# Latent attention: transposes two heads and value products five heads behind the logits, with probability tiles in the big pool

## The chip, the cores and the metric

The kernel runs on one core of a Trainium2 chip. The metric is the device time of one execution in microseconds; the number given is the median of several runs. A core has five engines with their own queues: TensorE (PE; its weight loads are listed as PEld), VectorE (DVE), ScalarE (ACT), GpSimd (POOL) and SyncE (SP), which here issues most DMAs.

## What is computed

Two transformer networks of two layers each, one behind the other, on 256 tokens of width 1024, in float32. The change touches one mixer of the second network, a latent attention with 16 heads, in which every query sees every key:

```python
def mla_mixer(h, pos, w_in, g_qa, w_qb, g_kva, w_kvb, g_q, g_k, w_o):
    proj = h @ w_in
    q_lat = proj[..., :Q_LORA]
    kv_lat = proj[..., Q_LORA:Q_LORA + KV_LORA]
    k_rope = rope(proj[..., Q_LORA + KV_LORA:], pos)
    q = (rms_norm(q_lat, g_qa) @ w_qb).reshape(B, S, MLA_HEADS, MLA_QK)
    kv = (rms_norm(kv_lat, g_kva) @ w_kvb).reshape(B, S, MLA_HEADS, MLA_NOPE + MLA_V)
    ...
    q = rms_norm(q, g_q)
    k = rms_norm(k, g_k)
    o = dense_attention(q, k, v, MLA_QK ** -0.5)
    return o.reshape(B, S, MLA_HEADS * MLA_V) @ w_o
```

`dense_attention` takes, for each head, the softmax of q k^T times the scale, and multiplies it with v. A query or key has 96 elements in a head (64 and 32 rotated ones), a value has 64. Ahead of this mixer lie the whole first network (two layers with a causal attention of 8 heads); behind it lie the output projection, an MLP, a second layer with a dilated attention, and a second MLP.

## The kernel before

All weights stream from HBM in chunks of up to 2112 columns (`raw`, four slots). ScalarE casts a chunk to its upper part (`whi`, L313), VectorE subtracts to get the lower part (`wlo`, L314), and every product with a weight is three matmuls (L362 to L364 with the weight as the moving side, L366 to L368 with it stationary).

Tiles come from pools with a fixed number of slots; a tile takes a slot until its last reader is done. `big` (`bt()`) has 32 slots, `t2()` has 5, `t1()` 6. In PSUM there are two pools of four banks: `acc()` for products with weights and for value products, `att()` for logits and transposes. A planner orders the work of each engine: every instruction has a rank by the place where the program lists it, and an instruction whose inputs or slots are not there yet may be passed by one of lower rank. The order so found is fixed in the program, and each engine then works its queue in that order.

The latent attention treats its 16 heads in four groups. For a group, `proj_kv` (L1317) and `proj_q` (L1347) project values, keys and queries, `post_kv` (L1338) scales keys, and `tr_qk` (L1367) transposes one head's queries and keys on TensorE (L1372) and copies them to a big tile on ScalarE (L1374, L1375). The attention itself is a generator, `attn_std` (L650), that is also used, with `causal` set, by the first network. It has three steps for a head:

- `st0`: logits (L674), row maximum (L677) and its scaling (L678) on VectorE, exponentials with row sums on ScalarE (L640, two of them), reciprocal (L643) and the normalising multiply (L648, two of them) on VectorE. The result is a probability tile `p`.
- `st1`: four transposes of `p` on TensorE (L695), copied by ScalarE to a tile `pt` (L697).
- `st2`, for a pair of heads: eight value-product instructions on TensorE (L707, L711) into one `acc` bank, whose two halves of the partitions belong to the two heads, and the split of the result on ScalarE (L479) and VectorE (L480) into `oT`.

The loop at L717 lists, at step i, `st0` of head i, `st1` of head i - D1 and, every second step, `st2` of the pair that begins at head i - D2. It stops after each (`yield`), and the driver (L1435) puts other work between: the projections and transposes of the next groups at fixed yields (L1431), two units of the modulation (`ada0`, at yields 20 and 30), and from yield 23 on one block each of the output projection (`out_ahead`, L1398; 21 blocks into three `acc` banks, a block only when its heads' `st2` is listed).

Big tiles alive in this stage: 8 of `oT`, 2 and 3 of the key-value and query latents (until the last group is projected), one value tile for each group, four query and key tiles for each group until its last `tr_qk`, one tile for each transposed head until its logits are done.

Of the kernel before, what the change touches and what calls it, by code (L numbers as in the profile page):

```python
# [240 lines left out]
def tile_net(ctx, tc, wts, ada, xin, cols_in, table_in, fb_in, c_in, pos_in, inv_in, mask_in, freq_in, out):  # L241
# [17 lines left out]
    def mk(pool, shape, dt, tag, bufs=None):  # L259
        cnt[0] += 1  # L260
        kw = {} if bufs is None else {"bufs": bufs}
        return pool.tile(shape, dt, tag=tag, name=f"{tag}{cnt[0]}", **kw)

    def bt(shape=(128, 512), dt=F32):
        return mk(big, list(shape), dt, "b")
# [7 lines left out]
    def t2(shape=(128, 512), dt=F32):  # L273
        return mk(t2p, list(shape), dt, "t2")

    def sm(n=1):
        return mk(smp, [128, n], F32, "sm")

    def acc():
        return mk(accp, [128, 512], F32, "acc")  # L280

    def att():
        return mk(attp, [128, 512], F32, "att")
# [194 lines left out]
    def split_plain(dst, src):  # L478
        S.copy(out=dst[:, 0, :], in_=src)  # L479
        V.tensor_tensor(out=dst[:, 1, :], in0=src, in1=dst[:, 0, :].bitcast(F32), op=ALU.subtract)  # L480
# [155 lines left out]
    def softmax_tail(src, spans, nm, P, qs=None, act=False):  # L636

        rs = sm(len(spans))
        for i, (a, b) in enumerate(spans):
            S.activation(out=P[:, a:b], in_=src[:, a:b], func=AF.Exp, bias=nm[:, i:i + 1], scale=1.0 if qs is None else qs[i],  # L640
                         accum_out=rs[:, i:i + 1])
        rc = sm(len(spans))
        V.reciprocal(out=rc[:, :len(spans)], in_=rs[:, :len(spans)])  # L643
        for i, (a, b) in enumerate(spans):
            if act:
                S.activation(out=P[:, a:b], in_=P[:, a:b], func=AF.Copy, scale=rc[:, i:i + 1])
            else:
                V.tensor_scalar(out=P[:, a:b], in0=P[:, a:b], scalar1=rc[:, i:i + 1], scalar2=None, op0=ALU.mult)  # L648

    def attn_std(heads, qkT, vcol, oT, causal, qscale=None, done=set()):  # L650


        P, PT, O = {}, {}, {}
        D1, D2 = (3, 6) if causal else (1, 4)

        def st0(h_):
            qk = qkT(h_)
            ps = att()
            nm = sm(2)
            p = t2()  # L660
            if causal:
                PE.matmul(out=ps[:, :128], lhsT=qk[:, 0, :128], rhs=qk[:, 1, :128], start=True, stop=True)
                PE.matmul(out=ps[:, 128:384], lhsT=qk[:, 0, 128:], rhs=qk[:, 1, :], start=True, stop=True)
                spans = [(0, 128), (128, 384)]
                sc = t2()
                mx = sm(2)
                for i, (a, b) in enumerate(spans):
                    V.tensor_tensor_reduce(out=sc[:, a:b], in0=ps[:, a:b], in1=cmask[:, 256 - (b - a):], scale=1.0,
                                           scalar=-3e38, op0=ALU.add, op1=ALU.max, accum_out=mx[:, i:i + 1])
                V.tensor_scalar(out=nm[:, :2], in0=mx[:, :2], scalar1=-1.0, scalar2=None, op0=ALU.mult)  # L670
                src = sc
            else:
                for i in range(2):
                    PE.matmul(out=ps[:, 256 * i:256 * i + 256], lhsT=qk[:, 0, 128 * i:128 * i + 128], rhs=qk[:, 1, :], start=True, stop=True)  # L674
                spans = [(0, 256), (256, 512)]
                mx = sm(2)
                V.tensor_reduce(out=mx[:, :2], in_=ps.rearrange("p (a b) -> p a b", a=2), axis=AX.X, op=ALU.max, negate=True)  # L677
                V.tensor_tensor(out=nm[:, :2], in0=mx[:, :2], in1=qscale(h_), op=ALU.mult)  # L678
                src = ps
            softmax_tail(src, spans, nm, p, None if causal else [qscale(h_)[:, i:i + 1] for i in range(2)], causal)  # L680
            P[h_] = p

        def st1(h_):
            p = P.pop(h_)
            ps = att()
            pt = t2()
            if causal:
                PE.transpose(ps[:, 0:128], p[:, 0:128], ident)
                PE.transpose(ps[:, 128:256], p[:, 128:256], ident)
                PE.transpose(ps[:, 256:384], p[:, 256:384], ident)  # L690
                S.copy(out=pt[:, :384], in_=ps[:, :384])
            else:
                for kt in range(2):
                    for qt in range(2):
                        PE.transpose(ps[:, kt * 256 + qt * 128:kt * 256 + qt * 128 + 128],  # L695
                                     p[:, qt * 256 + kt * 128:qt * 256 + kt * 128 + 128], ident)
                S.copy(out=pt, in_=ps)  # L697
            PT[h_] = pt

        def st2(h0):  # L700
            ps = acc()
            for kt in range(2):
                for e in range(2):
                    pt = PT[h0 + e]
                    o_ = ps[64 * e:64 * e + 64, :256]
                    if kt == 0:
                        PE.matmul(out=o_, lhsT=vcol(h0 + e, 0), rhs=pt[:, 0:256], start=True, stop=False)  # L707
                    elif causal:
                        PE.matmul(out=o_[:, 128:256], lhsT=vcol(h0 + e, 1), rhs=pt[:, 256:384], start=False, stop=True)
                    else:  # L710
                        PE.matmul(out=o_, lhsT=vcol(h0 + e, 1), rhs=pt[:, 256:512], start=False, stop=True)  # L711
            split_plain(oT[h0 // 2], ps[:, :256])
            done.add(h0 // 2)
            del PT[h0], PT[h0 + 1]

        n = len(heads)
        for i in range(n + D2):  # L717
            if i < n:
                st0(heads[i])
                yield 600  # L720
            if D1 <= i < n + D1:
                st1(heads[i - D1])
                yield 400
            if i >= D2 and (i - D2) % 2 == 0 and i - D2 < n:
                st2(heads[i - D2])
                yield 500
# [87 lines left out]
    for l in range(2):  # L814
# [70 lines left out]
        def attn_side(qa=qa, vt=vt, e2=e2, oT=oT, l=l):  # L885
            ps = att()
            PE.matmul(out=ps[:, 0:8], lhsT=upper, rhs=e2[:, 0:8], start=True, stop=True)
            PE.matmul(out=ps[:, 8:16], lhsT=ones, rhs=e2[:, 0:8], start=True, stop=False)
            PE.matmul(out=ps[:, 8:16], lhsT=upper, rhs=e2[:, 8:16], start=False, stop=True)
            for tt in range(2):  # L890
                for hf in range(2):
                    V.tensor_scalar(out=qa[1, tt, hf][:, :, 64:65].rearrange("p a b -> p (a b)"),
                                    in0=ps[:, 8 * tt + 4 * hf:8 * tt + 4 * hf + 4], scalar1=-1.0, scalar2=None, op0=ALU.mult)
            yield 1200
            qkT = {}
            for hd in range(8):
                qkT[hd] = bt([128, 2, 256])
            for hd in range(8):
                ps = att()
                for wh in range(2):  # L900
                    for tt in range(2):
                        PE.transpose(ps[:, wh * 256 + tt * 128:wh * 256 + tt * 128 + 128], qa[wh, tt, hd // 4][:, hd % 4, :], ident)
                S.copy(out=qkT[hd][:, 0, :], in_=ps[:, :256])
                V.tensor_scalar(out=qkT[hd][:, 1, :], in0=ps[:, 256:], scalar1=gA[:, l:l + 1], scalar2=None, op0=ALU.mult)
                yield 720
            yield from attn_std(list(range(8)), lambda hd: qkT[hd], lambda hd, kt: vt[kt][:, hd * 64:hd * 64 + 64], oT, True)
# [517 lines left out]
    for g in range(4):  # L1424
# [4 lines left out]
        if g + 1 < 4:  # L1429
            ops += [(5 + e, lambda g=g, e=e: tr_qk(4 * g + 4 + e)) for e in range(4)]  # L1430
        todo += [(8 * g + n_, f) for n_, f in ops]  # L1431
    at = attn_std(list(range(16)), lambda hd: qkM.pop(hd), lambda hd, kt: vM[hd // 4][:, kt, (hd % 4) * 64:(hd % 4) * 64 + 64], oT, False,
                  lambda hd: rM[hd // 4].rearrange("p (t a) -> p a t", t=2)[:, hd % 4, :], done)
    ahead, ahead_done = None, []
# [224 lines left out]
```

## Time and profile before

| what | us |
|---|---|
| median of 3 runs | 1575.91 (1574.87 to 1577.45) |
| the profiled execution's own time | 1573.53 |
| its span in the trace | 1571.8 |
| TensorE busy in the span | 1547.1 |
| TensorE at 2.4 GHz: mean granted clock | 0.999 |

The page lists busy times for each engine over the span, the chain of work that ended last, and groups of instructions by line, engine and tile. The views of the trace give the same for a stretch of time: busy time in windows, who waited for whom, and the instructions of one engine in order of time. An engine's idle time is put down to what ended it.

### The profile page before, as it was taken

How to read it: one execution, taken by the hardware profiler on the slowest of the kernel's cores; microseconds unless marked ns; L12 is line 12 of the kernel's file. 1: busy time of each engine (PE TensorE's matmuls, PEld its weight loads, DVE VectorE, ACT ScalarE, POOL GpSimd, SP SyncE). 2: the span in 40 equal slices, each digit the busy share in tenths (PEclk: the TensorE clock that was granted, in tenths of full speed). 3: DMA queues.
4: the chain of work that ended last, by engine and by line, in shares of the span. 5: the costliest groups of instructions: out<-in, count | busy, mean ns of one | idle time of the engine just before them, and what ended most of it. 6: DMA issues, size and time to landing. Idle time of an engine off the chain costs nothing.

```text
span 1571.8 us, 31232 instructions
## 1 busy us (share of the span) xinstructions
PE 1547.1 (98%) x12314; PEld 1502.6 (96%) x12314; DVE 1189.0 (76%) x2430; ACT 899.6 (57%) x1854; POOL 233.8 (15%) x273
## 2 busy tenths in 40 slices
PE   8999999999999999999989999999999999999999
PEld 7999999999899999999977899999999999999999
DVE  7877877789787777778878688767777777686642
ACT  7474554442657454443258677533676766677632
POOL 1100100055210010006312000010223222110000
PEclk9999999999999999999999999999999999999999
DMA  8455666644655666664534277776766667655551
GB/s 315 168 188 202 219 240 221 235 170 155 222 195 188 230 221 228 220 241 162 173 124 155 84 244 265 266 283 224 223 211 215 220 201 238 196 205 185 192 198 41
DMA packets 83906, 320.68 MB, mean 204 GB/s; under 512 B 31984, under 2 KB 34816, under 8 KB 58928
## 3 DMA queue, kind: packets, MB, share of 16 engines
q1 hardware_dynamic: 83184, 317.30, 58.9%
q8 instruction: 97, 1.59, 0.4%
q0 software_dynamic: 432, 1.28, 0.2%
q14 instruction: 49, 0.40, 0.1%
q10 hardware_dynamic: 144, 0.11, 0.0%
HBM read 311.32 MB, written 7.34 MB: 203 GB/s over the span
## 4 chain that ended last, share of the span: by engine, by line
PE 87%; DVE 8%; issue 2%; POOL 1%; ACT 1%; DMA 1%; SPq 0%; ACTq 0%; POOLq 0%; DVEq 0%
PE acc L366 20%; PE acc L368 20%; PE acc L367 20%; PE acc L362 6%; PE acc L364 6%; PE acc L363 6%; DVE wlo L314 3%; POOL sm L405 1%; PE att L1541 1%; PE att L1543 1%; PE att L1555 1%; DVE oh L743 1%; PE att L674 1%; PE acc L707 1%; PE att L1572 1%
## 5 line engine op out<-in xcount | busy, mean ns | idle before, releaser
L314 DVE TENSOR_TENSOR wlo<-raw,whi 128x1024 fp32r<-128x1024 f32 (+2 forms) x508 | 583.5, 1167 | 148.1 <-ACT whi L313 146.9
L313 ACT CAST whi<-raw 128x1024 fp32r<-128x1024 f32 (+2 forms) x508 | 495.3, 1000 | 312.0 <-PE acc L367 186.0
L366 PE MATMUL acc<-b,whi 128*128 128x256 f32 x1744 | 495.9, 285 | 2.3 <-ACT b L479 0.9
L367 PE MATMUL acc<-b,whi 128*128 128x256 f32 x1744 | 489.9, 281 | 0.0
L368 PE MATMUL acc<-b,wlo 128*128 128x256 f32 x1744 | 488.8, 280 | 0.0
L366 PE MATMUL acc<-h,whi 128*128 128x256 f32 (+1 forms) x1216 | 343.0, 282 | 0.0
L368 PE MATMUL acc<-h,wlo 128*128 128x256 f32 (+1 forms) x1216 | 342.3, 281 | 0.0
L367 PE MATMUL acc<-h,whi 128*128 128x256 f32 (+1 forms) x1216 | 341.3, 281 | 0.0
L366 PEld LDWEIGHTS acc<-b,whi 128*128 128x128 f32 x1744 | 328.1, 188 | 6.4 <-issue 3.2
L367 PEld LDWEIGHTS acc<-b,whi 128*128 128x128 f32 x1744 | 328.4, 188 | 1.2 <-issue 0.8
L368 PEld LDWEIGHTS acc<-b,wlo 128*128 128x128 f32 x1744 | 328.4, 188 | 0.1
L366 PEld LDWEIGHTS acc<-h,whi 128*128 128x128 f32 x1216 | 229.8, 189 | 0.0
L368 PEld LDWEIGHTS acc<-h,wlo 128*128 128x128 f32 x1216 | 229.1, 188 | 0.0
L367 PEld LDWEIGHTS acc<-h,whi 128*128 128x128 f32 x1216 | 229.0, 188 | 0.0
L362 PE MATMUL acc<-whi,h 128*128 128x384 f32 (+4 forms) x544 | 191.1, 352 | 2.4 <-ACT whi L313 2.4
L363 PE MATMUL acc<-wlo,h 128*128 128x384 f32 (+4 forms) x544 | 182.6, 336 | 0.7 <-DVE wlo L314 0.7
L364 PE MATMUL acc<-whi,h 128*128 128x384 f32 (+4 forms) x544 | 181.8, 336 | 0.0
L405 POOL TENSOR_TENSOR sm<-sm,mhalf 128x4 f32<-128x4 f32 (+3 forms) x72 | 92.1, 1279 | 378.4 <-DVE sm L404 353.6
L623 DVE CUSTOM_DVE_ANT_0 t<-raw,cond,cols 128x1024 bf16<-128x1024 f32 x96 | 121.8, 1280 | 6.1 <-PE att L690 3.4
L362 PEld LDWEIGHTS acc<-whi,h 128*128 128x128 f32 x544 | 102.2, 188 | 6.8 <-ACT whi L313 2.8
L363 PEld LDWEIGHTS acc<-wlo,h 128*128 128x128 f32 x544 | 102.6, 189 | 4.1 <-DVE wlo L314 1.3
L364 PEld LDWEIGHTS acc<-whi,h 128*128 128x128 f32 x544 | 102.0, 188 | 3.2 <-DVE h L1165 0.3
(256 smaller groups left out, 1730.4 us busy)
## 6 DMA issues: line engine op xcount, KB each, us to landing
raw<-in_wts_dram SPq DMA_DIRECT2D x194, 1024.0 KB, 4.8
raw<-in_ada_dram SPq DMA_DIRECT2D x48, 1024.0 KB, 4.9
raw<-in_wts_dram SPq DMA_DIRECT2D x50, 768.0 KB, 4.4
scr<-b SPq DMA_DIRECT2D x48, 128.0 KB, 4.6
b<-scr SPq DMA_DIRECT2D x64, 96.0 KB, 5.4
raw<-in_wts_dram SPq DMA_DIRECT2D x6, 576.0 KB, 3.9
raw<-in_wts_dram SPq DMA_DIRECT2D x6, 512.0 KB, 3.4
raw<-in_wts_dram SPq DMA_DIRECT2D x3, 528.0 KB, 4.8
```

The lines of the kernel that those rows point to most:

```text
L313: S.copy(out=hi[:, a:b], in_=r[:, a:b])
L314: V.tensor_tensor(out=lo[:, a:b], in0=r[:, a:b], in1=hi[:, a:b].bitcast(F32), op=ALU.subtract)
L362: PE.matmul(out=o_ap, lhsT=xhi, rhs=whi, start=start, stop=False)
L363: PE.matmul(out=o_ap, lhsT=xhi, rhs=wlo, start=False, stop=False)
L364: PE.matmul(out=o_ap, lhsT=xlo, rhs=whi, start=False, stop=stop)
L366: PE.matmul(out=o_ap, lhsT=whi, rhs=xhi, start=start, stop=False)
L367: PE.matmul(out=o_ap, lhsT=whi, rhs=xlo, start=False, stop=False)
L368: PE.matmul(out=o_ap, lhsT=wlo, rhs=xhi, start=False, stop=stop)
L405: G.tensor_tensor(out=r, in0=v[:, :n], in1=mhalf[:, :n], op=ALU.pow)
L623: V.tensor_tensor_reduce(out=junk, in0=w[:, e * 1024:e * 1024 + 1024], in1=cond, scale=1.0, scalar=col("ada_b", n), op0=ALU.mult, op1=ALU. ...
L674: PE.matmul(out=ps[:, 256 * i:256 * i + 256], lhsT=qk[:, 0, 128 * i:128 * i + 128], rhs=qk[:, 1, :], start=True, stop=True)
L707: PE.matmul(out=o_, lhsT=vcol(h0 + e, 0), rhs=pt[:, 0:256], start=True, stop=False)
```

## The change

For the attention that is not causal, the lags become 2 and 5 instead of 1 and 4, and the tiles `p` and `pt` come from `big` instead of `t2`. The causal attention stays as it is.

```diff
         P, PT, O = {}, {}, {}
-        D1, D2 = (3, 6) if causal else (1, 4)
+        D1, D2 = (3, 6) if causal else (2, 5)
 
         def st0(h_):
             qk = qkT(h_)
             ps = att()
             nm = sm(2)
-            p = t2()
+            p = t2() if causal else bt()
...
         def st1(h_):
             p = P.pop(h_)
             ps = att()
-            pt = t2()
+            pt = t2() if causal else bt()
```

## Rows read from the trace of the kernel before

**Rows 1.** The page: busy time of TensorE; engines on the chain that ended last.

```profile
PE 1547.1 (98%) x12314; PEld 1502.6 (96%) x12314; DVE 1189.0 (76%) x2430; ACT 899.6 (57%) x1854; POOL 233.8 (15%) x273
...
PE 87%; DVE 8%; issue 2%; POOL 1%; ACT 1%; DMA 1%; SPq 0%; ACTq 0%; POOLq 0%; DVEq 0%
```

**Rows 2.** Windows (stretch, length, busy of PE, PEld, DVE, ACT, POOL, clock, DMA): attention, next.

```profile
825.86:890.29 64.43, 60.59 (x367) 46.58 (x364) 47.29 (x150) 51.29 (x144) 8.72 (x6) 1.00 0.33 114
...
892.00:1000.00 108.00, 108.00 (x910) 108.00 (x909) 92.11 (x153) 80.61 (x187) 5.51 (x6) 1.00 0.73 251
```

**Rows 3.** Waits of TensorE, 826 to 892 us (total us, times, longest).

```profile
PE att L695 <- ACT b L1375: 1.4, 1, 1.4
PE att L695 <- DVE t L648: 0.8, 2, 0.5
PE acc L366 <- ACT b L479: 0.5, 1, 0.5
PE att L674 <- ACT t L640: 0.3, 1, 0.3
PE acc L366 <- DVE b L1343: 0.3, 1, 0.3
PE acc L362 <- DVE sm L404: 0.3, 1, 0.3
PE acc L707 <- ACT t L697: 0.3, 1, 0.3
```

**Rows 4.** Windows of 10 us in the attention, columns as in rows 2.

```profile
840.00:850.00 10.00, 8.27 (x49) 6.25 (x49) 8.52 (x20) 9.35 (x26) 0.03 (x1) 1.00 0.32 109
850.00:860.00 10.00, 9.35 (x57) 6.70 (x57) 8.82 (x33) 9.41 (x26) 3.27 (x2) 1.00 0.29 103
```

**Rows 5.** Groups by line, 826 to 892 us (busy us, mean ns, idle before).

```profile
L640 ACT ACTIVATE t<-att,sm,rq 128x256 f32<-128x256 f32 x32 | 17.8, 564 | 7.3 <-DVE sm L678 7.3
```

**Rows 6.** TensorE in order of time (start, us, instruction, idle before): up to the longest wait.

```profile
842.32 0.45 PE L362 MATMUL acc<-whi,b 128*128 128x384 f32 x1
...
847.59 1.03 PE L674 MATMUL att<-b 96*128 96x256 f32 x4
850.02 0.30 PE L695 MATMUL att<-ident,t 128*128 128x128 f32 x1 [1.41 <-ACT b L1375]
```

**Rows 7.** ScalarE in order of time, beside that wait.

```profile
848.14 0.56 ACT L640 ACTIVATE t<-att,sm,rq 128x256 f32<-128x256 f32 x1
...
848.69 0.58 ACT L697 COPY t<-att 128x512 f32<-128x512 f32 x1
...
849.41 0.49 ACT L1375 ACTIVATE b<-att,gM 96x256 f32<-96x256 f32 x1
```

**Rows 8.** TensorE in order of time: value products of a pair together and apart.

```profile
853.91 0.65 PE L707 MATMUL acc<-t,b 128*64 128x256 f32 x4
854.39 0.60 PE L711 MATMUL acc<-t,b 128*64 128x256 f32 x4
854.92 0.64 PE L1372 MATMUL att<-ident,b 128*96 128x128 f32 x4
...
862.18 0.65 PE L707 MATMUL acc<-t,b 128*64 128x256 f32 x2
862.75 0.39 PE L366 MATMUL acc<-b,whi 128*128 128x256 f32 x1
...
865.19 0.43 PE L707 MATMUL acc<-t,b 128*64 128x256 f32 x1
...
866.19 0.39 PE L367 MATMUL acc<-b,whi 128*128 128x256 f32 x1
```

**Rows 9.** VectorE in order of time: the row maxima of heads 8 and 15.

```profile
862.05 0.69 DVE L677 TENSOR_REDUCE sm<-att 128x2 f32<-128x512 f32 x1 [0.46 <-PE att L674]
...
883.14 0.69 DVE L677 TENSOR_REDUCE sm<-att 128x2 f32<-128x512 f32 x1 [0.65 <-PE att L674]
```

## Prediction

> **What bounds the kernel now.** I read the page first: TensorE is busy for 1547.1 of 1571.8 us, and the chain that ended last runs through it for 87% [rows 1]. So a saving counts only where it removes time in which TensorE stands still or works badly. The change touches one stage, the latent attention. I then read the windows: the stage runs from the projections of head group 2 at 825.86 us to the first block that needs the last heads' outputs at 890.29 us, 64.43 us long, with TensorE busy for 60.59 [rows 2]. Its idle time there is 3.84 us; the 108 us behind it have none [rows 2]. Third, the waits of TensorE in that stage, which the reader should add up: 1.4 for one bank of logits or transposes that ScalarE's head copies (L1375) had not emptied, 0.8 in two waits of the transposes for the normalised probabilities (L648), 0.5 and 0.3 at the tail, 0.3 three times elsewhere [rows 3]. That is all the change can take away openly: 3.8 us, 0.24% of the run. Last, the other engines: in the two slices in which most of the waits lie, ScalarE is busy for 9.35 and 9.41 of 10 us, VectorE for 8.52 and 8.82 [rows 4]. So around 840 to 860 us TensorE waits behind an engine that is nearly full itself.
>
> **The change part by part.** It adds and removes no instruction and no DMA. SP's and POOL's queues are passed by nothing: what moves is TensorE work, two ScalarE exponentials, a copy and small VectorE steps of each head, in the order that the planner is given.
>
> *Transposes two heads behind instead of one.* Head i's transposes are now ranked behind the logits of head i+2. The logits of a head are four instructions, 1.03 us [rows 6], and bring no extra work. The two waits for L648 arise because the transposes stand next in line while the normalising multiply of the same head still runs; the logits of another head now stand there. I take both at zero: 0.8 us gained. The bound on the other side is nothing gained, if the planner finds no logits ready there.
>
> *The 1.4 us wait.* TensorE issued head 5's logits at 847.59 for 1.03 us and then stood until 850.02, when head 4's transposes began [rows 6]. All four banks of that pool were taken: one by head 4's logits, which its second exponential released at 848.14 + 0.56 = 848.70; one by head 3's transposes, copied from 848.69; one by a head's query and key transposes, emptied at 849.41 + 0.49 = 849.90 [rows 7]; one by head 5's logits. Ranked first, the logits of head 6 could take the first free bank at 848.70 and run for four times about 0.22, until some 849.6; the transposes follow at 849.9 to 850.0. That recovers some 0.9 of 1.4 us. Bounds: 0, if ScalarE, full here, is simply the next thing that is late; 1.4 if the wait is gone.
>
> *Value products five instead of four heads behind.* The distance to the transposes is three in both versions, so a product waits for its probabilities as before. The last product is the 40th step of the list in both. The fill of the stage, 21 blocks of the output projection, is handed out from the same step on. I cost this at nothing; what hides it is that fill, and without it the tail waits of 0.3 and 0.5 [rows 3] stay. I leave both where they are, though with the last logits ranked two steps earlier the 0.3 could go.
>
> *Probability tiles in the big pool.* In program order the old lag wants six probability tiles at once from five slots (the logits of head 4 are listed before the products of heads 0 and 1), beside the query projection's squares. The new lag needs more, and in the big pool no such limit stands. But there it meets others. I counted live big tiles at head 5's logits: 8 output tiles, 2 + 3 latents, 3 value tiles, 8 query and key tiles of two groups, 2 transposed heads, 3 + 3 probabilities and their transposes: 32 of 32. Before, the peak of that count was 27. If a slot is late, an exponential waits on ScalarE, and behind it in the same queue the weight casts, the copies of transposes and those of queries and keys, for which TensorE waits. No row shows that wait. It costs 0 if slots come free as the count says, and one head's round if not: from the maximum of head 8 at 862.05 to that of head 15 at 883.14 it is 21.09 / 7 = 3.0 us a head [rows 9]. A gain is not excluded either, since the freed pool can bring the squares and the modulation's scratch forward, but both lie beside other work. I take 0, because in program order the count just fits.
>
> Sum: 0.8 + 0.9 = 1.7 us of the 3.8. The profiled execution took 1573.53 us around its span of 1571.8, so it would take about 1571.8; it lies 2.4 below the median of 1575.91. Against the median the forecast is 1574.2.
>
> **The rivals.** *Nothing moves.* The planner orders by readiness as well as by rank, and ScalarE at 94% in the slices concerned [rows 4] is what makes the banks late. Its work there is unchanged: the 32 exponentials of 564 ns wait for VectorE's scaling for 7.3 us in all [rows 5], and no part of the change shortens what VectorE does between. Then 1575.9.
>
> *More than the idle time.* A busy TensorE is not one at its best. A pair of heads' value products whose eight instructions stand together runs from 853.91 to 854.92, in 1.01 us, since the two heads work side by side. Where only the first head's tile was ready they stand apart: 862.18 to 862.75 for two, and 865.19 to 866.19 for the other six, 1.57 us [rows 8]. Of the eight pairs four are split so. With two heads in flight the probabilities of a pair come closer together; if all four pairs closed up, 4 x 0.56 = 2.2 us would be saved that no idle row shows, and with most waits gone too (2.6 of 3.8) the gain is 4.8: 1571.1. Against it: the distance from transposes to products is unchanged, and that distance decides which tile is ready.
>
> The Trainium skill's page "Perfetto Trace Analysis" (Identifying the Most-Contended Engine) points the same way: it says to judge TensorE by the time of its weight loads and not by matmul time. By that measure the stage has 64.43 - 46.58 = 17.9 us of room [rows 2], and the sum would be several times mine. The trace bears this out only in part: each logits matmul streams for about 0.22 us under a load that ends sooner, so much of that gap is shape and not room. The same page (Optimization Strategy) says that regular bubbles can mean that the memory for the next tile is short, which is what the bank wait of 1.4 us looks like, though it comes once.
>
> *Slower: the big pool is full.* If the planner runs projections of group 3 ahead, as the kernel before does (those of the queries begin at 842.32, head 5's logits come at 847.59 [rows 6]), their tiles take slots early; with up to four transposed probability tiles alive, I count 34 wanted against 32. An exponential is then held until a pair of products is done. One such hold of 3.0 us costs 1.3 net of the gain and stays within the bound below; it needs two holds with no fill, 6.0 - 1.7 = 4.3 us, to be slower: 1580.2. Speaking for it: the fill is listed only from yield 23 on, when eleven heads' logits are listed, so little covers TensorE before that. Against it: a late projection tile of group 3 has three groups of slack.
>
> **How the numbers follow.** Forecast (1.7 us gained) 0.44; nothing moves 0.22; more than the idle time 0.22; the big pool 0.12. A measurement of this kernel can tell about 0.2%, 3.15 us, from no change: the bounds are 1572.8 and 1579.1. The forecast and "nothing moves" lie between them. Faster takes the third case and a little of the forecast's upper side, 0.25; slower takes most of the last, 0.12; same 0.63. The range runs from the third case to one hold of the pool (1575.9 + 1.3 = 1577.2), each with the runs' own spread (1.0 below and 1.5 above their median): 1570.1 to 1578.7. Beyond it lie the last case and the far end of the third.
>
> **What would show it.** In the profile after: TensorE's waits in the stage without L648, with the L1375 row under 0.5, and about 2.1 us in all instead of 3.84; the stage near 62.7 us long; the value products split as often as before. "More than the idle time" would show seven or eight pairs whole and a stage under 60 us. A full pool would show ScalarE's exponential or a query or key copy waiting for a TensorE or VectorE step of an older head, and a longer stage. I am wrong if the stages after it change length: nothing in them is touched, but the planner lays out the whole program.

## The result and the profile after

The changed kernel takes 1586.33 us (median of 4, 1584.02 to 1587.50) against 1575.46 of the kernel before on the same chip: a ratio of 1.0062, 95% interval 1.0047 to 1.0076. It is slower by 0.6% (10.9 us between the medians). The forecast was 1574.2 us, a gain of 1.7 us that could hardly be told from no change. The profiled execution took 1586.72 us around a span of 1585.0, 13.2 longer than the span of before.

The page after, TensorE's busy time and the chain that ended last (columns as in [rows 1]):

```profile
PE 1553.4 (98%) x12314; PEld 1508.9 (95%) x12314; DVE 1188.9 (75%) x2430; ACT 899.4 (57%) x1854; POOL 234.6 (15%) x273
...
PE 85%; DVE 8%; ACT 2%; issue 2%; DMA 2%; POOL 1%; SPq 0%; ACTq 0%; POOLq 0%; DVEq 0%
```

The counts of instructions are the same on every engine. TensorE is busy for 6.3 us more, so 6.9 of the 13.2 us are idle time and the rest is slower work: ahead of the last 2 us the kernel after has five stretches of 3.4 us at half the granted clock, the kernel before has one (789.0 to 792.4 us).

To find the place, I compared the start times of the same instructions in both traces. The kernel after is 1.2 us late when the attention's first logits begin, 9.8 us late at its end, and 2.9 us more are lost at 1102 to 1108 us. The first 1.2 us arise in the first 44 us of the run, which the change does not touch: one of the stretches at half clock lies there (13.0 to 16.4 us). Fifteen of the twenty traces have one at this place, that of `crowded` below among them; the trace of before has none. From here on "the stage" is the time from the first logits to the last value product. Windows of it, before and then after (columns as in [rows 2]):

```profile
828.53:889.45 60.92, 57.54 (x353) 44.49 (x351) 44.59 (x138) 48.25 (x135) 6.55 (x4) 1.00 0.31 104
```

```profile
829.75:899.05 69.30, 59.31 (x346) 45.11 (x344) 45.07 (x138) 48.31 (x135) 6.54 (x4) 0.95 0.26 92
```

The stage is 8.4 us longer: 6.6 more of idle TensorE (9.99 against 3.38) and 1.8 more of busy time, at a mean granted clock of 0.95 instead of 1.00. The other engines do the same work in it as before. TensorE's waits in the stage after, to be held against [rows 3] (total us, times, longest):

```profile
PE acc L707 <- DVE t L1255: 2.8, 2, 1.5
PE att L695 <- ACT b L640: 2.4, 2, 2.2
PE att L695 <- DVE b L648: 1.5, 1, 1.5
PE att L1372 <- ACT b L640: 1.5, 2, 0.9
PE acc L362 <- DVE t L1255: 0.9, 1, 0.9
PE att L674 <- ACT b L640: 0.5, 1, 0.5
PE acc L366 <- DVE b L1343: 0.3, 1, 0.3
```

The wait of 1.4 us for the key copy (L1375) and the two waits for L648 between 835 and 847 us are gone, as forecast. But a new wait for L648, of 1.5 us, stands at the tail: head 15's transposes wait for its multiply, and no logits are left to stand in between. The other new waits are 4.4 us for exponentials (L640) and 3.7 us for the query rotation on VectorE (L1255), the last reader of an `acc` bank. Nearly all of these come in two clusters. TensorE in order of time, the two clusters and the tail:

```profile
836.17 1.03 PE L674 MATMUL att<-b 96*128 96x256 f32 x4
837.03 0.60 PE L695 MATMUL att<-ident,b 128*128 128x128 f32 x4
838.51 0.64 PE L1372 MATMUL att<-ident,b 128*96 128x128 f32 x4 [0.88 <-ACT b L640]
840.61 0.62 PE L707 MATMUL acc<-b,b 128*64 128x256 f32 x2 [1.46 <-DVE t L1255]
842.10 0.57 PE L362 MATMUL acc<-whi,b 128*128 128x512 f32 x1 [0.87 <-DVE t L1255]
...
853.71 1.03 PE L674 MATMUL att<-b 96*128 96x256 f32 x4
...
855.57 1.13 PE L674 MATMUL att<-b 96*128 96x256 f32 x4
...
860.07 0.65 PE L707 MATMUL acc<-b,b 128*64 128x256 f32 x4 [1.35 <-DVE t L1255]
...
863.34 1.12 PE L695 MATMUL att<-ident,b 128*128 128x128 f32 x4 [2.18 <-ACT b L640]
...
895.24 0.30 PE L695 MATMUL att<-ident,b 128*128 128x128 f32 x1 [1.52 <-DVE b L648]
```

What VectorE does meanwhile, in order of time (L677 is a head's row maximum, L314 a weight split, L1329 to L1360 the drain of a group's projections):

```profile
835.75 0.67 DVE L677 TENSOR_REDUCE sm<-att 128x2 f32<-128x512 f32 x1
...
837.39 1.23 DVE L314 TENSOR_TENSOR wlo<-raw,whi 128x1024 fp32r<-128x1024 f32 x1 [0.37 <-ACT whi L313]
...
838.61 0.40 DVE L1329 TENSOR_REDUCE sm<-t 128x4 f32<-128x256 f32 x1
...
842.03 0.68 DVE L677 TENSOR_REDUCE sm<-att 128x2 f32<-128x512 f32 x1
...
855.03 0.40 DVE L1329 TENSOR_REDUCE sm<-t 128x4 f32<-128x256 f32 x1
...
857.78 1.23 DVE L314 TENSOR_TENSOR wlo<-raw,whi 128x1024 fp32r<-128x1024 f32 x1 [0.79 <-ACT whi L313]
...
861.03 0.68 DVE L677 TENSOR_REDUCE sm<-att 128x2 f32<-128x512 f32 x1
```

Read the two together. Head 3's logits are done at 837.20, and their maximum starts at 842.03: a weight split and the whole drain of group 2's projections stand before it in VectorE's queue. Head 6's logits are done at 854.74, and their maximum starts at 861.03, behind group 3's drain. Until the maximum is taken, no exponential of that head can run, so its logits keep their bank, and TensorE stands before the next transposes: these are the waits for L640. The waits for L1255 are for `acc` banks that the drain frees late. The drain itself starts late: head 2's softmax, whose logits now stand ahead of the projections, takes its place on VectorE first (the drain begins 8.9 us after the first logits, before 6.2 us after them). VectorE before, with the start of group 2's drain and the maxima of heads 2 and 6, which stand behind a drain there too:

```profile
834.77 0.40 DVE L1329 TENSOR_REDUCE sm<-t 128x4 f32<-128x256 f32 x1
...
838.20 0.68 DVE L677 TENSOR_REDUCE sm<-att 128x2 f32<-128x512 f32 x1
...
855.07 0.69 DVE L677 TENSOR_REDUCE sm<-att 128x2 f32<-128x512 f32 x1
```

After both clusters the granted clock falls. Windows after (columns as in [rows 2]): the first cluster, the stretch behind it, the next one, and the stretch behind the second cluster:

```profile
839.15:842.40 3.25, 0.92 (x4) 0.49 (x4) 3.25 (x16) 1.82 (x4) 1.81 (x2) 1.00 0.25 103
842.45:845.80 3.35, 3.35 (x11) 1.92 (x10) 3.33 (x11) 2.63 (x8) 1.41 (x1) 0.50 0.20 17
845.90:856.00 10.10, 9.74 (x58) 7.71 (x55) 4.67 (x13) 6.36 (x19) 0.00 (x0) 1.00 0.25 101
862.95:866.25 3.30, 2.91 (x10) 1.80 (x10) 3.30 (x9) 1.38 (x6) 0.00 (x0) 0.50 0.02 7
```

TensorE was busy for 0.92 of the 3.25 us before the clock fell from 2.4 to 1.2 GHz. While it is down, the weight matmuls of 512 columns start 0.43 us apart instead of 0.23.

The 2.9 us at 1102 us, far behind the change (VectorE, then TensorE):

```profile
1098.35 1.28 DVE L623 CUSTOM_DVE_ANT_0 t<-raw,cond,cols 128x1024 bf16<-128x1024 f32 x1 [2.45 <-DMA raw<-in_ada_dram]
```

```profile
1102.50 0.61 PE L447 MATMUL att<-ones,t 128*128 128x2 f32 x4 [2.00 <-DVE t L441]
```

A step of the modulation waits 2.45 us for its data on VectorE, a norm behind it is late, and TensorE waits 2.00 us there; before, that wait was 0.61. Another stretch of 3.4 us at half clock follows (1105.2 to 1108.6 us). The kernels with parts of the change lose 0 to 3.9 us at this place. I did not find its cause.

### The profile page after: what moved, and what is told of

Its sections match the earlier page's. It is cut to its first block, busy times and chain, and to the rows that moved or that the text cites. A ratio compares the mean times of both kernels' runs of the same rounds, so it can differ in the third digit from the quotient of the medians.

```text
span 1585.0 us, 31236 instructions
## 1 busy us (share of the span) xinstructions
PE 1553.4 (98%) x12314; PEld 1508.9 (95%) x12314; DVE 1188.9 (75%) x2430; ACT 899.4 (57%) x1854; POOL 234.6 (15%) x273
## 4 chain that ended last, share of the span: by engine, by line
PE 85%; DVE 8%; ACT 2%; issue 2%; DMA 2%; POOL 1%; SPq 0%; ACTq 0%; POOLq 0%; DVEq 0%
PE acc L366 20%; PE acc L368 20%; PE acc L367 20%; PE acc L362 6%; PE acc L363 6%; PE acc L364 6%; DVE wlo L314 3%; DMA raw<-in_ada_dram 1%; PE att L1541 1%; POOL sm L405 1%; PE att L1543 1%; PE att L1555 1%; DVE oh L743 1%; PE att L674 1%; PE att L1572 1%
## 5 line engine op out<-in xcount | busy, mean ns | idle before, releaser
L314 DVE TENSOR_TENSOR wlo<-raw,whi 128x1024 fp32r<-128x1024 f32 (+2 forms) x508 | 582.6, 1165 | 148.0 <-ACT whi L313 146.6
```

The lines of the kernel that those rows point to most:

```text
L314: V.tensor_tensor(out=lo[:, a:b], in0=r[:, a:b], in1=hi[:, a:b].bitcast(F32), op=ALU.subtract)
```

## The experiments

The theories, by the letters that the expectations use. A: the third head's softmax stands ahead of the projections' drain on VectorE, and `acc` banks come free late. B: the big pool is crowded. C: the end of that drain, wherever it comes from, sets the next weight products. D: the row maxima stand behind drains and splits in VectorE's fixed order, logits hold their banks, and exponentials and TensorE wait for that. E: two heads in flight cost something anywhere in the stage.

**The parts alone.** `lags_only` has the lags 2 and 5 with the tiles in `t2`; `pool_only` the old lags with the tiles in `big`; the other two have the big pool and one lag each.

```diff
-        D1, D2 = (3, 6) if causal else (1, 4)
+        D1, D2 = (3, 6) if causal else (2, 5)   # lags_only
-            p = t2()
+            p = t2() if causal else bt()        # pool_only, and the same for pt
-        D1, D2 = (3, 6) if causal else (2, 5)
+        D1, D2 = (3, 6) if causal else (2, 4)   # transposes_only, from the kernel after
+        D1, D2 = (3, 6) if causal else (1, 5)   # products_only, from the kernel after
```

> The lags of 2 and 5 alone; the probability tiles stay in the pool of five. Theory A (the lag: the softmax of a third head is listed ahead of the drain of the group's projections on VectorE, the four acc banks come free late, TensorE stands and its clock falls): most of the loss stays, 1582 to 1587, with TensorE waiting for L1255 near 840 and 860 us. Theory B (the probability tiles crowd the big pool): the loss is gone, 1574 to 1577. The five slots could blunt the lag itself; then something between.

> The probability tiles in the big pool alone, with the lags of before, 1 and 4. Theory A: no loss, 1572 to 1577. Theory B: most of the loss, 1582 to 1587.

> Transposes two heads behind, value products four heads behind as before, tiles in the big pool. Theory A: the loss comes with the transposes' lag, 1582 to 1587. If it came with the products' lag instead, 1573 to 1577. Theory B: a little less than the full loss, since fewer tiles are alive, 1578 to 1586.

> Transposes one head behind as before, value products five heads behind, tiles in the big pool. Theory A: no loss, 1572 to 1577, TensorE's waits in the stage under 5 us. Theory B: as many tiles in the big pool as before or one more than with the lags of before, so a loss, 1580 to 1586.

| kernel | ratio to before (95%) | stage, us | idle TensorE in it | logits waiting for their maximum, heads 2 to 7 / 8 to 15 |
|---|---|---|---|---|
| before | 1 | 60.9 | 3.4 | 9.8 / 1.7 |
| pool_only | 1.0025 (1.0016 to 1.0035) | 64.3 | 7.5 | 13.7 / 2.4 |
| products_only | 1.0041 (1.0028 to 1.0053) | 69.1 | 11.1 | 19.7 / 2.2 |
| lags_only | 1.0044 (1.0027 to 1.0062) | 67.5 | 7.5 | 18.7 / 10.4 |
| after | 1.0062 (1.0047 to 1.0076) | 69.3 | 10.0 | 22.1 / 4.7 |
| transposes_only | 1.0070 (1.0049 to 1.0092) | 73.2 | 9.7 | 21.3 / 3.6 |

The last column adds, over the heads, the time from the end of a head's logits on TensorE to the start of its maximum on VectorE, both read from the engines in order of time. The columns from the stage on are from one execution each, the ratio is from all. The pool alone costs 0.25%, the lags alone 0.44%; on top of the pool the lag of the products costs 0.16%, that of the transposes 0.45% and both together 0.37%. So each part costs time, and they do not simply add up. A expected the time of `lags_only` rightly and those of `pool_only` and `products_only` wrongly; B had `products_only` right and the other two wrong; `transposes_only` came out above both. `pool_only` loses in a way of its own; its waits of TensorE in the stage begin with one that before has once, for 0.5 us and behind the stage [rows 3], and after not at all:

```profile
PE acc L366 <- ACT b L479: 2.6, 3, 0.9
PE att L674 <- ACT b L640: 2.1, 2, 1.5
```

The fill waits three times for the split of a value product on ScalarE. Why the pool alone leads there stays open.

**The big pool's room.** The kernel before, with five big tiles taken through the whole attention.

```diff
+    held = [bt() for _ in range(5)]
...
+    hj = sm(1)
+    for t_ in held:
+        G.tensor_tensor(out=hj[:, :1], in0=t_[:, 0:1], in1=oT[7][:, 0, 0:1].bitcast(F32), op=ALU.add)
```

> The kernel before with five more tiles of the big pool taken through the whole attention, so that my count peaks at 32 of 32 while probability tiles stay in their own pool. Theory B (the loss of the tiles in the big pool comes from its being full): 1578 to 1582. Rival (it comes from the probability tiles no longer being held back by five slots, so that softmaxes run ahead): 1574 to 1577.5, the order of work unchanged.

1575.74 us, ratio 1.0003 (0.9993 to 1.0013), stage 60.96: no difference with 32 of 32 tiles taken by my count. The 34 that my slower rival wanted were not tried. But in the kernel after no longer wait of an exponential in the stage ends with a reader of an older head's tile: 16.9 us of these waits end with VectorE's scaling (L678) and 1.3 with the step behind it (L632). And `lags_only` loses without a probability tile in the big pool. So B falls, and with it the mechanism of my slower rival.

**The place of the projections and their drain.** The projections of groups 2 and 3 are listed at a yield after each group's start. `proj_early` (from after) lists them at 1 instead of 2, `before_proj_late` (from before) at 3; `before_drains` (from before) ranks the first readers of their banks (squares, sums, copies, rotation) far ahead.

```diff
-            ops += sorted([(2, 0, lambda g=g: proj_kv(g + 2)), (5, 1, lambda g=g: post_kv(g + 2)), (2, 2, lambda g=g: proj_q(g + 2))], key=lambda z: z[:2])
+            ops += sorted([(1, 0, lambda g=g: proj_kv(g + 2)), (5, 1, lambda g=g: post_kv(g + 2)), (1, 2, lambda g=g: proj_q(g + 2))], key=lambda z: z[:2])
...
-            sq = t1()
-            S.activation(out=sq, in_=akv[tt][:, :256], func=AF.Square)
+            with tc.high_priority(400):
+              sq = t1()
+              S.activation(out=sq, in_=akv[tt][:, :256], func=AF.Square)
...
```

> The changed kernel, with the projections of each next group listed one yield earlier, so that those of group 2 stand ahead of the logits of head 2 again, as they do with the lags of before. Theory A (a third head's softmax in front of the drain of the projections on VectorE holds the acc banks): TensorE's stall near 840 us is gone, the one near 860 may stay, 1579 to 1584 against some 1586 for the changed kernel. Rival (the tiles' pool, or the lag in itself, wherever the projections stand): 1585 to 1588.

> The kernel before, lags 1 and 4 and the pool of five, with the projections listed one yield later, behind the logits of head 2. Theory A: the stall near 840 us appears without any change of lag or pool, 1578 to 1582, TensorE waiting for L1255 or for an exponential there for 2 us or more. Rival: the small pool holds the softmaxes back anyway, 1574 to 1577.5.

> The kernel before with the readers of the projections' acc banks (squares, copies, sums, rotation) ranked 400 places higher. Theory A: the acc banks come free earlier and TensorE's waits in the stage shrink from 3.8 us to 1 to 3 us, 1572.5 to 1576. Rival (softmaxes are then late by as much): 1576 to 1580.

`before_proj_late`: 1580.02 us, ratio 1.0023 (1.0013 to 1.0032), stage 64.0. With neither lag nor pool touched, the mere place of the projections in the list costs 3 us, the time that A expected, though TensorE's wait near 841 us is 1.6 us for ScalarE's squares (L1358) and not one that A named. And `proj_early` should then have given most of the loss back, and took 1587.09, ratio 1.0067 (1.0051 to 1.0083): A does not carry. `before_drains` took 1583.67, ratio 1.0049 (1.0033 to 1.0065): drains that go first cost the kernel before 7 us, more than either theory expected, and its logits of heads 2 to 7 wait 12.4 us for their maxima instead of 9.8.

**Key scaling earlier.** `post_kv` of groups 2 and 3 is listed at yield 2 instead of 5, so that the key banks drain earlier; in the kernel after and in the kernel before.

```diff
-            ops += sorted([(2, 0, lambda g=g: proj_kv(g + 2)), (5, 1, lambda g=g: post_kv(g + 2)), (2, 2, lambda g=g: proj_q(g + 2))], key=lambda z: z[:2])
+            ops += sorted([(2, 0, lambda g=g: proj_kv(g + 2)), (2, 1, lambda g=g: post_kv(g + 2)), (2, 2, lambda g=g: proj_q(g + 2))], key=lambda z: z[:2])
```

> The changed kernel with the keys' scaling of a group, which empties the two acc banks of its key-value projection, listed with the projection and not three yields later. Theory C (the loss is the late drain of the projections on VectorE: while their acc banks are held, neither the next projection nor the 21 blocks of fill can start, and TensorE stands): the last scaling of group 3 ends at some 30 to 34 us after the first logits instead of 38.4, the first fill comes with it, and the time falls to 1577 to 1583 from some 1586. Rival (the lag costs the same wherever the drain stands, since each head's chain through three engines is what is long): 1584 to 1588.

> The kernel before with the keys' scaling listed with the projection: banks free earlier. Theory C: the last scaling of group 3 ends before 28 us after the first logits and the fill starts earlier, 1572 to 1577. Rival: softmaxes are late by as much, 1576 to 1580.

`post_early` took 1589.51, ratio 1.0087 (1.0070 to 1.0104): group 3's bank is free 32.4 us after the first logits instead of 38.4, and all the same the stage is 4.7 us longer than that of the changed kernel. So C falls: an earlier drain does not shorten the stage. `before_post_early` took 1583.22, ratio 1.0051 (1.0035 to 1.0067), with the lags and pool of before. Both lie above what either side expected. VectorE of `before_post_early` in order of time:

```profile
838.06 0.42 DVE L1343 TENSOR_TENSOR b<-acc,sm 128x256 f32<-128x256 f32 x1 [1.36 <-POOL sm L405]
...
840.79 0.68 DVE L677 TENSOR_REDUCE sm<-att 128x2 f32<-128x512 f32 x1
```

The key scaling waits 1.36 us for a root on GpSimd, and head 2's maximum, whose logits were ready, waits behind it; heads 2 to 7 wait 24.2 us in all. Work that is put ahead of the maxima on VectorE costs the same kind of time without any change of lag: this led to D.

**A shorter drain.** The rotation of the queries of groups 2 and 3 is left out on VectorE, with a copy on ScalarE in its place; from after and from before.

```diff
-            rope_to(qb[:, :, 64:96], q3[:, :, 64:96], tt, t1([128, 4, 32]), 4)
+            if g < 2:
+                rope_to(qb[:, :, 64:96], q3[:, :, 64:96], tt, t1([128, 4, 32]), 4)
+            else:
+                S.copy(out=qb[:, :, 64:96], in_=q3[:, :, 64:96])
```

> The changed kernel without the rotation of the queries of groups 2 and 3 on VectorE (ScalarE copies them unrotated; four VectorE instructions for each of four halves are left out). Theory C: the drain ends 2 us earlier in each of two groups, banks and fill come earlier, 1579 to 1584. Rival (chain of each head): 1584 to 1588.

> The kernel before, without the same rotation: the price of that work where TensorE hardly stands. Theory C: the wait of 0.3 for the bank in front of group 3's projection and that in front of the fill may go, 1573 to 1577; the distance between the two kernels without rotation is then half of the distance with it. Rival: the distance stays at 10 us.

1586.21 (1.0066, 1.0049 to 1.0082) and 1576.34 (1.0009, 1.0000 to 1.0019): nothing gained in either, and the distance of 10 us stays, as the rival expected. In `after_norope` heads 6 and 7 still wait 6.4 and 8.6 us for their maxima, so a drain shorter by this piece is not enough.

**The maxima of heads 3 and 6 ahead of the drains.** From after: the VectorE part of the projections of groups 2 and 3 is cut off, listed behind those heads' logits and issued after their maximum.

```diff
-                V.tensor_reduce(out=mx[:, :2], in_=ps.rearrange("p (a b) -> p a b", a=2), axis=AX.X, op=ALU.max, negate=True)
+                lastmax[0] = V.tensor_reduce(out=mx[:, :2], in_=ps.rearrange("p (a b) -> p a b", a=2), axis=AX.X, op=ALU.max, negate=True)
...
+    def drains2(a, b):
+        with tc.issue_after(lastmax[0].ins):
+            next(a)
+            next(b)
```

> The changed kernel with the order of VectorE bound in two places: the drain of group 2's projections is issued behind the row maximum of head 3, that of group 3's behind that of head 6. Theory D (logits wait in the four att banks for maxima that stand behind the drain; transposes wait for those banks): the exponentials come earlier, TensorE's waits for L640 in the stage fall from 4.4 us to under 1.5, and the time to 1577 to 1583. Theory C would have it slower, since the acc banks come free later: 1587 to 1592. An effect of the lag in itself: 1584 to 1588.

1587.08 us, ratio 1.0067 (1.0052 to 1.0082): no gain, against what D expected of it; the time lies where an effect of the lag in itself was put. The two maxima did come early (8.9 and 24.9 us after the first logits, instead of 12.3 and 31.3). VectorE and TensorE of this kernel (here the maximum is L679, its scaling L680):

```profile
863.75 0.68 DVE L679 TENSOR_REDUCE sm<-att 128x2 f32<-128x512 f32 x1
864.35 1.22 DVE L314 TENSOR_TENSOR wlo<-raw,whi 128x1024 fp32r<-128x1024 f32 x1
865.48 0.15 DVE L680 TENSOR_TENSOR sm<-sm,rq 128x2 f32<-128x2 f32 x1
```

```profile
866.99 1.09 PE L1388 MATMUL att<-ident,b 128*96 128x128 f32 x4 [3.64 <-ACT b L640]
```

The wait has moved one head on. Head 7's maximum now stands behind the drain, its scaling of 0.15 us behind one more weight split, and TensorE waits 3.64 us. Here the repair of one place in the order handed the delay to the next. It also shows the limit of the last column of the table above: heads 2 to 7 of this kernel wait only 11.7 us for their maxima, and its stage is 70.7 us long all the same, for the scaling behind the maximum counts as well.

**No maxima at all.** Both kernels without the row maxima and their scaling, with logits scaled by 0.05 so that the exponentials stay in range: 13 us of VectorE's work (16 times 0.68 and 0.15) and the whole path through VectorE between logits and exponentials are taken out.

```diff
-            nm = sm(2)
+            nm = sm(2) if causal else None
...
-                V.tensor_reduce(out=mx[:, :2], in_=ps.rearrange("p (a b) -> p a b", a=2), axis=AX.X, op=ALU.max, negate=True)
-                V.tensor_tensor(out=nm[:, :2], in0=mx[:, :2], in1=qscale(h_), op=ALU.mult)
```

> The changed kernel without the row maxima and their scaling in the latent attention (logits made twenty times smaller, so that the exponentials need no maximum): logits go to ScalarE straight and no bank waits for VectorE. Theory D: most of the loss is gone, 1572 to 1579, with the distance to the kernel before without maxima under 4 us. The lag in itself: the distance stays near 10 us.

> The kernel before, without the row maxima in the same way: what the shorter chain gives where TensorE stands for 3.8 us only. Both theories: 1571 to 1576; it is the measure for after_nomax.

1573.67 (ratio 0.9985, 0.9976 to 0.9995) and 1570.63 (0.9963, 0.9948 to 0.9978). The change now costs 3.0 us instead of 10.9 by the medians; by the two intervals taken together the rest lies between 0.7 and 6.3 us. TensorE's waits in the stage of `after_nomax`:

```profile
PE att L696 <- ACT b L641: 2.2, 1, 2.2
PE acc L366 <- DVE b L1344: 0.4, 1, 0.4
PE acc L362 <- DVE t L1256: 0.4, 1, 0.4
PE acc L708 <- DVE t L1256: 0.3, 1, 0.3
```

Of the two clusters one wait is left. The stage takes 58.2 us against 56.3 in `before_nomax`, at a granted clock of 1.00 in both: 1.9 us more instead of 8.4. So most of the loss needs VectorE between logits and exponentials. The pair does not separate the position of the maxima from the 13 us of work that went with them.

**One bank more for weight products.** From after: five banks for `acc`, three for `att`.

```diff
-    accp = ctx.enter_context(tc.tile_pool(name="accp", bufs=4, space=PS))
-    attp = ctx.enter_context(tc.tile_pool(name="attp", bufs=4, space=PS))
+    accp = ctx.enter_context(tc.tile_pool(name="accp", bufs=5, space=PS))
+    attp = ctx.enter_context(tc.tile_pool(name="attp", bufs=3, space=PS))
```

> The changed kernel with five acc banks and three att banks in place of four and four. Theory D: slower still, 1588 to 1600, since one bank fewer holds logits and transposes. Theory C: faster, 1577 to 1583.

1596.06 us, ratio 1.0121 (1.0105 to 1.0138), stage 71.9. Taking a bank from the logits costs more than one for the projections gives. But against the kernel after 4.7 us are lost ahead of the attention, so only the stage's 2.6 us bear on D.

**The change by place.** `change_late` is the kernel before for heads 0 to 7 and makes the whole change, lags and pool, from head 8 on; `change_early` does the reverse. In the kernel before, the last group's drain ends at 855.1 us and head 8's logits begin at 861.0, so the border between the two lies behind the drains. The loop is rewritten so that no head is listed twice or left out where the lags change.

```diff
+            if not causal:
+                D1, D2 = (2, 5) if i >= 8 else (1, 4)   # change_late; i < 8 in change_early
...
+            p = bt() if not causal and h_ >= 8 else t2()   # and the same for pt
```

> Kernel before for heads 0 to 7, the whole change (lags 2 and 5, probability tiles in the big pool) from head 8 on. Theory D (the loss is that logits wait for VectorE's row maximum while the drains of the projections of groups 2 and 3 stand on it; in the kernel after, heads 2 to 7 wait 22.1 us in all between the end of their logits and the start of their maximum, against 9.8 before, heads 8 to 15 only 6.4 against 3.0): 1574 to 1578, and the stage from the first logits to the last value product 60 to 63 us. Rival E (two heads in flight cost their banks at any place, also beside the fill, or the list of the tail is worse): 1579 to 1584, with stalls for exponentials behind the first block of the fill. A gain of more than 2 us is expected by neither, because the kernel before has only some 0.6 us of idle TensorE behind the first block.

> The whole change for heads 0 to 7 and the order and tiles of before from head 8 on. Theory D: the whole of the loss or nearly all, 1582 to 1588, stage 66 to 72 us, heads 6 and 7 wait over 8 us in all for their row maxima, and TensorE's clock falls to half at least once in the stage. Rival E: the loss is halved, 1578 to 1582.

(The 6.4 and 3.0 us in the first of these texts contain 1.5 us of heads 0 and 1; the traces give 6.2 and 3.2.) `change_late` took 1576.75, ratio 1.0005 (0.9995 to 1.0015), with a stage of 62.0 us; `change_early` took 1583.89, ratio 1.0054 (1.0041 to 1.0066), with a stage of 69.5. The first half carries the loss; the second half carries none that can be measured. The waits of `change_early` on TensorE stand as in the kernel after, almost to the hundredth:

```profile
839.31 0.64 PE L1377 MATMUL att<-ident,b 128*96 128x128 f32 x4 [0.88 <-ACT b L640]
841.42 0.62 PE L707 MATMUL acc<-b,b 128*64 128x256 f32 x2 [1.46 <-DVE t L1260]
842.91 0.79 PE L362 MATMUL acc<-whi,b 128*128 128x512 f32 x1 [0.87 <-DVE t L1260]
...
860.63 0.65 PE L707 MATMUL acc<-b,b 128*64 128x256 f32 x4 [1.36 <-DVE t L1260]
863.89 1.11 PE L695 MATMUL att<-ident,b 128*128 128x128 f32 x4 [2.18 <-ACT b L640]
```

In `change_late` the maxima of heads 8 to 15 wait 8.8 us in all instead of 1.7, and the stage grows by only 1.1: beside the output projection's fill, late maxima cost little. Heads 2 to 7 of `change_late` wait 9.8 us as in the kernel before, those of `change_early` 22.0 as in the kernel after. E falls as far as the time can tell. One cost of the lag itself does show: the wait of 1.5 us for L648 at the tail, which `change_late` has as the kernel after has it, and `change_early` has not.

What is settled: the loss comes from heads 0 to 7, while the projections of groups 2 and 3 drain through VectorE, and most of it goes with the row maxima and their work. What stays open: whether their place in VectorE's order or their work is what costs, why each single reorder of VectorE left the time where it was or made it longer, how lag and pool share the loss, the 3.0 us that remain without maxima, and the loss at 1102 us. One rival was not tested: `pool_only`, `before_proj_late`, `before_drains` and `before_post_early` keep the old lags, move only the kernel's own work or tiles, and cost 0.23 to 0.51% each, so part of the loss may be that of any step away from an order that happens to fit. No kernel that computes everything was faster than the kernel before.

## Why the prediction was wrong

*What bounds the kernel* held: TensorE, with 3.8 us of openly idle time. Reading this as the only amount at stake was a mistake: it tells what can be gained openly, and not what an unfavourable order can cost.

*Transposes two heads behind, 0.8 us gained.* This is the step that failed. The two waits for L648 went, and so did the first wait of [rows 3], but a wait of 1.5 us for L648 came at the tail, and `transposes_only` against `pool_only` puts the price of this lag at 0.45%, some 7 us. I wrote that the logits of another head "bring no extra work" and asked only what TensorE finds to do. A head's logits bring a row maximum, a scaling, a reciprocal and two multiplies on VectorE and hold a bank until VectorE gets to them. [rows 4] had VectorE at 8.52 and 8.82 of 10 us there, and I read ScalarE's 9.35 beside it as the limit. VectorE's order in the two critical stretches was not read row by row; it shows the drain of a group as one block ahead of a maximum already before (838.20 for head 2, 855.07 for head 6). With one more head in flight heads 2 to 7 wait 22.1 instead of 9.8 us for their maxima, and TensorE waits for exponentials behind them. `change_early` shows the place; the kernels without maxima show that most of the loss goes with the maxima; that their place behind the drains is the reason is argued from the order of time, and `max_ahead`, which moved two of them, gained nothing.

*The wait of 1.4 us, 0.9 gained.* It went as a row, and the transposes came to wait for an exponential instead: 2.18 us at 863.34.

*Value products five heads behind, at nothing.* `products_only` against `pool_only` costs 0.16%: the step is not free. I had named the fill as its cover; the fill begins only behind the place where the loss lies.

*Tiles in the big pool, at nothing.* The bounds were one hold of 3.0 us or none. `crowded` shows that 32 tiles found room; `pool_only` still cost 0.25%, 3.9 us, outside my forecast for this term. The rival on the slower side had the sign right and the mechanism wrong, and its price of 4.3 us was less than half of the loss.

*TensorE's clock* had no term in the sum, because the granted clock of before is 1.00 in every window of the stage [rows 2, 4]. Two stretches at half of it go with the 1.8 us of added busy time. A range built from idle rows alone is too short on the slower side when a stall of 3 us brings a slow stretch behind it.

*What would show it.* The L1375 row is gone, and L648 is gone from its two old places (not from the stage: 1.5 us at the tail), in a stage that got longer. So these are signs that the edit took effect on those waits, and not that it gained. The sum of the waits (2.1 us forecast, 9.9 seen) and the length of the stage were the signs that counted. Of the eight pairs of value products three stood apart. Before it was five: I had counted the four that begin with two instructions, and of the pair at 877.20 the last two come at 879.67. So at my price of 0.56 us a pair "more than the idle time" had some 1.1 of its 2.2 us. The remark that a change in later stages would prove me wrong was right by its wording: 2.9 us were lost at 1102 us.

## What to carry to other kernels

A deeper software pipeline asks for one more result in flight from every engine that the step passes through, and each of these results keeps its PSUM bank until the slowest of them has read it: before ranking work earlier on one engine, list what it puts into the queue of the others, and what stands ahead of it there. Removing a named wait is no gain in itself where the engine behind it is 85% busy; read that engine's order in the critical stretch and follow one bank from its first write to its last reader. Put such a change where other work covers it: from head 8 on, the same edit cost nothing that could be measured.

## What the runs showed of the hardware that was not expected

Stalls of TensorE can cost more than their length. After the cluster at 839 to 842 us (busy 0.92 of 3.25 us) the granted clock stood at 1.2 GHz for 3.4 us, and 512-column matmuls took some 630 ns instead of some 395. Most kernels with such a cluster show stretches like this in the stage, of 3.4 or 6.8 us each and in `transposes_only` of 13.7; `lags_only` has two, `change_early` one of 3.4 and one of 6.8. `pool_only` and `before_post_early`, whose idle time of 7.5 and 8.5 us comes in pieces of at most 1.5 and 1.8 us, apart from each other, have none. The length of a piece alone does not tell: `before_proj_late` has such a stretch behind a wait of 1.6 us.
